# Low parts of the input weights made by an accumulating transfer in an encoder block on one core

## The chip, the core and the metric

The kernel runs on one core of one Trainium2 chip. A core has TensorE (PE in the profile, PEld for its weight loads), VectorE (DVE), ScalarE (ACT), GpSimd (POOL) and SyncE (SP), each with its own in-order instruction queue, and 16 transfer (DMA) engines that they share. The metric is the device time of one execution in microseconds; of several runs the median counts.

## The reference

One layer of a hybrid encoder block on 1,024 tokens of 1,024 channels, in float32:

```python
hn = rms_norm(h, ln_g[l])
proj = hn @ w_in[l] + b_in[l]            # 1024 -> 3584
glu_a, glu_b, z_conv, q, k, v, z_att = jnp.split(proj, cuts, axis=-1)
y_conv = conformer_conv(glu_a, glu_b, dw_w[l], ...)   # 31 taps, LayerNorm, swish, 512x512
y_att = neighbourhood_attention(q, k, v, rpb[l])      # 8 heads, window 8 x 16 on a 16 x 64 grid
y_conv = grouped_rms_norm(y_conv, ...) * silu(z_conv)
y_att = grouped_rms_norm(y_att, ...) * silu(z_att)
h = h + concatenate([y_conv, y_att]) @ w_out[l]
return rms_norm(h, final_g)
```

## The kernel before

Every large product is made in three matmuls of rounded operands (type fp32r): a float32 operand is split into a high part, its rounding, and a low part, the rest, and high x high + high x low + low x high are summed in PSUM (`proj`, L368). The split input `hi`, `lo` of the 1,024 tokens stays in SBUF.

The input projection is cut into 28 chunks of 128 output channels. A chunk's weights are 1,024 x 128 numbers, 512 KB. `prefetch` (L337) walks the chunks in the order `order` (L208): the first nine are the lead (three pairs for the gated linear unit of the convolution, then q, k and v of the first pair of heads), then come those that are worked in between attention blocks, and at the end two final gates (chunks 27 and 28 of the order). For each chunk it loads the raw weights from HBM on SP's queue (`wraw`, L210; eight pieces of 512 B for each partition), rounds them on ScalarE into the high part `wh` in two instructions of four 128-column blocks (KS = 4, L47), and subtracts on GpSimd, also in two instructions, to make the low part `wl` (`low_weight`, L355). There is one raw buffer (`r_raw`) and there are two buffers each for `wh` and `wl` (`r_w`), so a chunk's high part can be written when the last matmul of the chunk before the last one is done. The raw buffer is returned when the second subtraction is planned to end.

The program's order on every engine is written by a planner at build time (`Clock`, L95; `weave`, L110). It keeps a modelled time, adds a modelled cost for every instruction, and lets generators of higher priority go first whenever their modelled inputs are ready. The GpSimd subtractions wait in a list `jobs` and are issued when GpSimd's modelled queue is free. `ready[n]` holds a chunk's two tiles and the modelled time at which each of its eight blocks may be used; `weight` (L362) waits for it, and `proj` for each block's time. The taps of the depthwise convolution (`taps`, L470: one VectorE instruction a tap, with two operands in SBUF) fill VectorE wherever its modelled queue is empty. The real engines only keep the order, not the times.

`final_gates` (L1034) takes the last two chunks together: for each of the eight blocks the six matmuls of the one, then the six of the other. The output projection reads what the gates give, and its buffers are those that the gates release.

Of the kernel before, what the change touches and what calls it, by code (L numbers as in the profile page):

```python
# [9 lines left out]
F32 = mybir.dt.float32  # L10
F32R = mybir.dt.float32r
AF = mybir.ActivationFunctionType
ALU = mybir.AluOpType
# [4 lines left out]
P = 128  # L18
D = 1024
T = 1024  # L20
NK = D // P
# [25 lines left out]
KS = 4  # L47
# [7 lines left out]
QI = 0.1  # L55
LW = 10.9
SQ_DVE = (4,6)


def mk(t, offset, dims):  # L60
# [88 lines left out]
def block(ctx: ExitStack, tc: tile.TileContext, x, vecs, w_in, dw_w, pw_w, pw_b, rpb, w_out, final_g, out):  # L149
    nc = tc.nc  # L150
    pool = lambda name, bufs, **k: ctx.enter_context(tc.tile_pool(name=name, bufs=bufs, **k))
# [12 lines left out]
    ck = Clock(nc)  # L164
    ring = lambda n: Ring(ck, n)
    r_u, r_raw, r_w, r_x, r_uh, r_ul, r_gz, r_y = ring(16), ring(1), ring(2), ring(XB), ring(1), ring(0), ring(1), ring(1)
# [41 lines left out]
    order = [c + int(f[1:]) for f in LEAD + FILL for c in of[f[0]]] + [CH_ZC + 3, CH_ZA + 3]  # L208

    def wraw(n):  # L210
        c = order[n]
        raw = wrp.tile([P, NK, P], F32, tag="wr", name=f"wr{c}")
        nc.sync.dma_start(out=raw, in_=w_in[0][:, c * P:(c + 1) * P].rearrange("(k p) n -> p k n", p=P))
        return raw

    def wtiles(n):
        c = order[n]
        return (whp.tile([P, NK, P], F32R, tag="wh", name=f"wh{c}"),
                wlp.tile([P, NK, P], F32R, tag="wl", name=f"wl{c}"))

    for t in range(4):
        xload(t)
    raw0 = wraw(0)
    for t in range(4, NT):
        xload(t)
# [37 lines left out]
    def x_tile(t):  # L263
        yield land[t]
        ss = sm.tile([P, 1], F32, tag="ss", name=f"ss{t}")
        rs = sm.tile([P, 1], F32, tag="rs", name=f"rs{t}")
        eng = "dve" if t in SQ_DVE else "act"
        while t >= 4 and ck.q[eng] > ck.now + QI:
            yield ck.now + 0.1
        if t in SQ_DVE:  # L270
            e = ck.dve("scalar_tensor_tensor", out=acc[:, t % 4, :], in0=xt[t], scalar=1.0 / 1024.0, in1=xt[t],
# [57 lines left out]
    ready = {}  # L329
# [7 lines left out]
    def prefetch():  # L337
        for n in range(len(order)):
            if n < W_AHEAD or "pw" in state:
                yield from r_raw.get()  # L340
                raw, end = (wraw(n), ck.now + 4.0) if n else (raw0, land_w)
                yield from r_w.get()
            else:
                yield from r_w.get()
                yield from r_raw.get()
                raw, end = wraw(n), ck.now + 4.0
            whi, wlo = wtiles(n)
            yield end
            for k0 in range(0, NK, KS):
                kk = slice(k0, k0 + KS)  # L350
                t = ck.act(out=whi[:, kk, :], in_=raw[:, kk, :], func=AF.Copy)
                ck.jobs.append((t, partial(low_weight, n, raw, whi, wlo, kk)))
                yield

    def low_weight(n, raw, whi, wlo, kk):  # L355
        k = dict(out=wlo[:, kk, :], in0=raw[:, kk, :], in1=whi[:, kk, :].bitcast(F32), op=ALU.subtract)
        t = ck.gps("tensor_tensor", 0.1 + 0.0022 * KS * P, **k)
        ready.setdefault(n, (whi, wlo, []))[2].extend([t] * KS)
        if kk.stop == NK:
            r_raw.put(t)  # L360
# [628 lines left out]
    ck.spawn(all_turned(), 0)  # L989
    ck.spawn(tap_cols(), -1)  # L990
    ck.spawn(prefetch(), -1)
    ck.spawn(bias_rows(), 2)
    ck.spawn(lead(), 5)
# [221 lines left out]
_VECS = ["ln_g", "b_in", "dw_b", "cln_g", "cln_b", "gn_conv_g", "gn_att_g"]  # L1215
# [20 lines left out]
```

## Time and profile before

| | us |
|---|---|
| median of 3 runs | 571.23 (568.81 to 573.75) |
| the profiled execution | 572.21 |
| its span, first to last instruction | 570.4 |
| TensorE busy | 539.3 |
| VectorE busy | 412.2 |
| ScalarE busy | 260.1 |
| GpSimd busy | 195.1 |

TensorE's mean granted clock is 0.992 of full speed. Busy time is counted by instruction records; matmuls overlap, so one record of 0.39 us stands for about 0.23 us of progress where they follow each other closely. In the rows below a line gives the start and the duration in us, the engine, the line of the kernel, the operation, output and inputs, and in brackets the idle time before it and what ended that. L127, L131, L136, L140 and L144 are the helpers that record every matmul, transpose, activation, VectorE and GpSimd instruction, so groups go by the names of the tiles.

### The profile page before, as it was taken

To read this page: it belongs to the slowest core of one execution; us is meant where nothing else is said; L and a number is where in the kernel's file an instruction comes from. 1 tells how busy PE (TensorE), PEld (TensorE's weight loads), DVE (VectorE), ACT (ScalarE), POOL (GpSimd) and SP (SyncE) were. 2 spreads that over 40 slices of the span, in tenths; PEclk is the share of its full clock that TensorE was granted. 3 is DMA by queue.
4 is the path that set the end of the run, shared out by engine and by line. 5 is a ranking of instruction groups with operands and counts; after the bars stand their busy time and mean duration, and the time that the engine had idled before them with its cause. 6 is when DMAs were issued, how large, how long until landed. Compare 5 with 4: busy or idle time off the path is not lost.

```text
span 570.4 us, 7827 instructions
## 1 busy us (share of the span) xinstructions
PE 539.3 (95%) x2717; PEld 447.2 (78%) x2717; DVE 412.2 (72%) x665; ACT 260.1 (46%) x634; POOL 195.1 (34%) x176
## 2 busy tenths in 40 slices
PE   4999999898999998999997999999999999999995
PEld 3688888676888886888786788788888888888885
DVE  4747999987999979988999884667564365464232
ACT  6552221124555153655465645875665555253121
POOL 7513543232222343232525152542515552031121
PEclk9999999998999999999998999999999999999999
DMA  9413546663123442263241241101101470044221
GB/s 330 145 14 84 168 128 223 172 192 111 40 57 103 125 105 66 74 149 103 65 142 54 77 120 46 38 26 52 39 0 38 158 284 0 2 148 145 78 75 74
DMA packets 62331, 57.74 MB, mean 101 GB/s; under 512 B 9981, under 2 KB 51765, under 8 KB 62292
## 3 DMA queue, kind: packets, MB, share of 16 engines
q1 hardware_dynamic: 62222, 57.22, 33.6%
q8 instruction: 21, 0.34, 0.3%
q14 instruction: 18, 0.15, 0.1%
q10 hardware_dynamic: 70, 0.03, 0.0%
HBM read 36.58 MB, written 11.58 MB: 84 GB/s over the span
## 4 chain that ended last, share of the span: by engine, by line
PE 71%; DVE 17%; DMA 4%; issue 3%; ACT 2%; SPq 2%; POOL 1%; POOLq 0%; ACTq 0%; DVEq 0%
PE out L127 15%; PE pz L127 13%; DVE acc L140 12%; PE pv L127 6%; PE pk L127 6%; PE pq L127 5%; PE po L127 4%; PE pw L127 4%; PE pb L127 4%; PE ptp L131 3%; PE pa L127 3%; PE s L127 3%; DMA kl<-kl 1%; PE po L131 1%; DMA x<-in_x 1%
## 5 line engine op out<-in xcount | busy, mean ns | idle before, releaser
L140 DVE SCALAR_TENSOR_TENSOR acc<-glu,dwc,acc 128x512 f32<-128x512 f32 (+25 forms) x150 | 186.7, 1270 | 1.2
L144 POOL TENSOR_TENSOR wl<-wr,wh 128x512 fp32r<-128x512 f32 x56 | 93.9, 1695 | 153.0 <-ACT wh L136 147.7
L127 PE MATMUL pz<-hi,wh 128*128 128x512 f32 x128 | 52.2, 408 | 0.0
L127 PE MATMUL out<-wol,yh 128*128 128x512 f32 (+1 forms) x136 | 51.2, 377 | 0.0
L127 PE MATMUL out<-woh,yl 128*128 128x512 f32 (+1 forms) x136 | 51.2, 377 | 0.0
L127 PE MATMUL out<-woh,yh 128*128 128x512 f32 (+1 forms) x136 | 51.2, 377 | 0.0
L127 PE MATMUL pz<-hi,wl 128*128 128x512 f32 x128 | 50.3, 393 | 0.1
L127 PE MATMUL pz<-lo,wh 128*128 128x512 f32 x128 | 50.1, 391 | 0.0
L136 ACT ACTIVATE wh<-wr 128x512 fp32r<-128x512 f32 x56 | 32.3, 628 | 30.5 <-DMA wr<-in_w_in 20.9
L140 DVE TENSOR_TENSOR ptl<-ptp,pth 128x512 fp32r<-128x512 f32 x64 | 37.0, 614 | 1.2 <-ACT pth L136 1.2
L136 ACT ACTIVATE pth<-ptp 128x512 fp32r<-128x512 f32 x64 | 31.8, 543 | 13.2 <-PE ptp L131 12.4
L140 DVE CUSTOM_DVE_ANT_0 s<-s,bias 128x264 f32<-128x264 f32 (+1 forms) x64 | 30.2, 512 | 7.3 <-PE s L127 4.2
L140 DVE TENSOR_TENSOR xr<-out,xr 128x512 f32<-128x512 f32 (+1 forms) x17 | 11.1, 660 | 33.6 <-PE out L127 29.1
L136 ACT ACTIVATE prob<-s,mx 128x264 f32<-128x264 f32 (+1 forms) x64 | 33.6, 536 | 0.6 <-DVE mx L140 0.4
L136 ACT ACTIVATE os<-po 128x256 f32<-128x256 f32 x32 | 12.4, 387 | 41.9 <-PE po L127 41.8
L131 PE MATMUL ptp<-ident,prob 128*128 128x128 f32 x224 | 30.0, 273 | 0.0
L127 PE MATMUL pq<-hi,wh 128*128 128x512 f32 x64 | 26.6, 416 | 3.2 <-DVE v L140 3.2
L127 PE MATMUL po<-pth,v 128*128 128x256 f32 x112 | 29.5, 291 | 0.0
L144 POOL TENSOR_TENSOR ams<-ams,mhalf 128x8 f32<-128x8 f32 x8 | 14.6, 1819 | 43.5 <-DVE ams L140 43.5
L127 PE MATMUL po<-ptl,v 128*128 128x256 f32 x112 | 29.3, 290 | 0.0
L127 PEld LDWEIGHTS out<-woh,yh 128*128 128x128 f32 x136 | 25.6, 188 | 4.7
L127 PEld LDWEIGHTS out<-woh,yl 128*128 128x128 f32 x136 | 25.6, 188 | 4.7
(153 smaller groups left out, 1371.0 us busy)
## 6 DMA issues: line engine op xcount, KB each, us to landing
wr<-in_w_in SPq DMA_DIRECT2D x28, 512.0 KB
x<-in_x SPq DMA_DIRECT2D x8, 512.0 KB
wor<-in_w_out SPq DMA_DIRECT2D x8, 512.0 KB
xr<-in_x SPq DMA_DIRECT2D x8, 512.0 KB
out<-xr SPq DMA_DIRECT2D x16, 256.0 KB
kh<-kh SPq DMA_DIRECT2D x24, 128.0 KB
kl<-kl SPq DMA_DIRECT2D x24, 128.0 KB
q<-ql SPq DMA_DIRECT2D x16, 128.0 KB
```

The costliest lines, as they stand in the source:

```text
L127: self.nc.tensor.matmul(out, lhsT=lhsT, rhs=rhs, start=start, stop=stop)
L131: self.nc.tensor.transpose(out=out, in_=in_, identity=identity)
L136: self.nc.scalar.activation(**k)
L140: getattr(self.nc.vector, fn)(**k)
L144: getattr(self.nc.gpsimd, fn)(**k)
```

## The change

For the first three chunks nothing changes but the layout. From the fourth chunk on the raw buffer is returned right after the high part; ScalarE writes the negated high part into the low part's buffer, in two more instructions; and a transfer issued by GpSimd reads the chunk's weights from HBM a second time and adds them to that buffer. The planner is told 0.95 us for the issue and 5.8 us more until all eight blocks can be used. The host lays the weights out so that each partition of a chunk is one piece of 4 KB. The issue of the transfer goes to the head of the list `jobs`.

```diff
+N_SUB = 3
@@ wraw
-        nc.sync.dma_start(out=raw, in_=w_in[0][:, c * P:(c + 1) * P].rearrange("(k p) n -> p k n", p=P))
+        nc.sync.dma_start(out=raw, in_=w_in[c])
@@ prefetch
                 t = ck.act(out=whi[:, kk, :], in_=raw[:, kk, :], func=AF.Copy)
-                ck.jobs.append((t, partial(low_weight, n, raw, whi, wlo, kk)))
+                if n < N_SUB:
+                    ck.jobs.append((t, partial(low_weight, n, raw, whi, wlo, kk)))
                 yield
+            if n < N_SUB:
+                continue
+            r_raw.put(t)
+            for k0 in range(0, NK, KS):
+                kk = slice(k0, k0 + KS)
+                t = ck.act(out=wlo[:, kk, :], in_=whi[:, kk, :].bitcast(F32), func=AF.Copy, scale=-1.0)
+                yield
+            ck.jobs.insert(0, (t, partial(low_added, n, whi, wlo)))
+
+    def low_added(n, whi, wlo):
+
+        nc.gpsimd.dma_start(out=wlo, in_=w_in[order[n]], accum_op=ALU.add)
+        t = max(ck.q["pool"], ck.now) + 0.95
+        ck.q["pool"] = t
+        ready[n] = (whi, wlo, [t + 5.8] * NK)
@@ kernel
+    w_in = np.asarray(inputs["w_in"])[0].reshape(NK, P, -1, P).transpose(2, 1, 0, 3)
```

## Rows read from the trace of the kernel before

**Rows 1.** The page's parts 1 and 4: busy time by engine; the chain's shares.

```profile
PE 539.3 (95%) x2717; PEld 447.2 (78%) x2717; DVE 412.2 (72%) x665; ACT 260.1 (46%) x634; POOL 195.1 (34%) x176
...
PE 71%; DVE 17%; DMA 4%; issue 3%; ACT 2%; SPq 2%; POOL 1%; POOLq 0%; ACTq 0%; DVEq 0%
```

**Rows 2.** Timeline of TensorE, the waits for VectorE's results between 100 and 310 us.

```profile
101.17 0.49 PE L127 MATMUL pk<-hi,wh 128*128 128x512 f32 x1 [0.85 <-DVE ql L140]
...
108.55 0.50 PE L127 MATMUL pk<-hi,wh 128*128 128x512 f32 x1 [1.63 <-DVE ql L140]
...
127.32 0.36 PE L127 MATMUL s<-kl,q 128*128 128x264 f32 x1 [1.42 <-DMA kl<-kl]
...
220.56 0.48 PE L127 MATMUL pq<-hi,wh 128*128 128x512 f32 x1 [2.12 <-DVE v L140]
...
278.61 0.47 PE L127 MATMUL pq<-hi,wh 128*128 128x512 f32 x1 [1.07 <-DVE v L140]
...
307.56 1.09 PE L131 MATMUL ln<-ident,acc 128*128 128x128 f32 x8 [2.27 <-DVE ptl L140]
```

**Rows 3.** Busy time by stretch: PE, PEld, DVE, ACT, POOL, PEclk, DMA share, GB/s.

```profile
136.00:138.00 2.00, 2.00 (x7) 1.56 (x6) 2.00 (x7) 1.54 (x6) 0.00 (x0) 0.53 0.96 263
...
310.00:312.00 2.00, 1.62 (x6) 1.62 (x7) 1.93 (x7) 1.22 (x4) 0.72 (x2) 0.51 0.00 0
```

**Rows 4.** Chain (taps); GpSimd's timeline; stretch 45 to 345, low parts alone.

```profile
47.66 1.28 DVE acc L140
...
48.96 2.19 DVE acc L140
...
48.21 4.09 POOL L144 TENSOR_TENSOR wl<-wr,wh 128x512 fp32r<-128x512 f32 x2 [4.47 <-ACT wh L136]
...
45.00:345.00 300.00, 68.23 (x38) 0.99 0.41 113
```

**Rows 5.** Groups by line: busy us, mean ns of one | idle before.

```profile
L144 POOL TENSOR_TENSOR wl<-wr,wh 128x512 fp32r<-128x512 f32 x56 | 93.9, 1695 | 153.0 <-ACT wh L136 147.7 <-DMA row<-abn 5.2
...
L136 ACT ACTIVATE wh<-wr 128x512 fp32r<-128x512 f32 x56 | 32.3, 628 | 30.5 <-DMA wr<-in_w_in 20.9 <-PE pq L127 4.9 <-PE pz L127 4.6
```

**Rows 6.** Timelines of SP and ScalarE, two weight loads; then stretches as in rows 3.

```profile
43.77 0.40 SPq L213 DMA_DIRECT2D wr<-in_w_in  x1
...
47.50 1.15 ACT L136 ACTIVATE wh<-wr 128x512 fp32r<-128x512 f32 x2 [1.45 <-DMA wr<-in_w_in]
...
124.41 0.53 SPq L213 DMA_DIRECT2D wr<-in_w_in  x1
...
130.69 1.15 ACT L136 ACTIVATE wh<-wr 128x512 fp32r<-128x512 f32 x2 [4.18 <-DMA wr<-in_w_in]
...
43.00:48.00 5.00, 5.00 (x24) 4.14 (x23) 1.84 (x3) 1.19 (x2) 0.74 (x1) 1.00 0.41 110
...
455.00:460.00 5.00, 4.90 (x22) 3.70 (x21) 2.48 (x3) 3.66 (x7) 3.62 (x3) 1.00 1.04 415
```

**Rows 7.** Timelines, two chunks: high part's start and first matmul with the low part.

```profile
57.42 1.15 ACT L136 ACTIVATE wh<-wr 128x512 fp32r<-128x512 f32 x2 [0.49 <-DMA wr<-in_w_in]
...
67.37 0.39 PE L127 MATMUL pb<-hi,wl 128*128 128x512 f32 x1
...
279.63 1.15 ACT L136 ACTIVATE wh<-wr 128x512 fp32r<-128x512 f32 x2 [1.26 <-DMA wr<-in_w_in]
...
287.37 0.39 PE L127 MATMUL pz<-hi,wl 128*128 128x512 f32 x1
```

**Rows 8.** Timelines, the last chunk: high part, low part, first matmul with it.

```profile
454.30 1.15 ACT L136 ACTIVATE wh<-wr 128x512 fp32r<-128x512 f32 x2 [2.61 <-PE pz L127]
...
455.01 2.54 POOL L144 TENSOR_TENSOR wl<-wr,wh 128x512 fp32r<-128x512 f32 x2 [6.34 <-ACT wh L136]
...
456.36 0.51 PE L127 MATMUL pz<-hi,wl 128*128 128x512 f32 x1
```

**Rows 9.** The accumulator's instructions: duration ns min/median/max, first and last start.

```profile
L140 DVE TENSOR_SCALAR acc<-glu,dwc,cols x5: 535/802/811, 46.8 to 278.4; 128x1024 f32<-128x1024 f32 x3, 128x512 f32<-128x512 f32 x2
```

More of the change, by code (lines that the diff above doesn't have):

```diff
@@ L1224 @@
     nc = bacc.Bacc("TRN2", target_bir_lowering=False, num_devices=1)
-    inputs = dict(inputs, vecs=np.concatenate([np.asarray(inputs[n])[0].reshape(-1, P) for n in _VECS]))
+    w_in = np.asarray(inputs["w_in"])[0].reshape(NK, P, -1, P).transpose(2, 1, 0, 3)
+    inputs = dict(inputs, w_in=w_in, vecs=np.concatenate([np.asarray(inputs[n])[0].reshape(-1, P) for n in _VECS]))
     arrays, args = {}, []
```

## The prediction

> **What bounds the kernel now.** I read the page's first part first: TensorE is busy for 539.3 of 570.4 us, VectorE for 72% and the other engines for less [rows 1]. The chain that ended last lies on TensorE for 71% and on VectorE for 17% [rows 1]. So an edit moves the end only where TensorE stands still or runs at its lower clock, and the next view is the list of TensorE's waits in order of time. In the middle of the run they are waits for VectorE: 0.85 and 1.63 us for the low half of q, 1.42 us for copies of the low half of k (which VectorE writes), then 2.12, 1.07 and 2.27 us for v and for a low half of the probabilities [rows 2]. After two groups of such waits the granted clock is 0.53 and 0.51 of full speed, that is the 1.2 GHz level [rows 3]. Nothing there waits for a weight.
>
> The third view is VectorE's part of the chain, read beside GpSimd's timeline. A full-length convolution tap takes 1.28 us by itself, and 2.19 us where it runs beside the weights' low-part subtraction on GpSimd [rows 4]. The subtraction reads two operands from SBUF, and so does a tap. One pair of subtractions (4.09 us) hits two taps, which is 2 x 0.91 = 1.8 us of VectorE. Between 45 and 345 us, while the taps run, there are 38 subtractions, 19 pairs [rows 4]: up to 19 x 1.8 = 34 us of VectorE time in which it falls behind the order that the planner wrote.
>
> **Removed: 50 subtractions on GpSimd.** They are 50 of the 56 at a mean of 1.70 us, 85 us of GpSimd [rows 5], off the path by themselves. What counts is what they do to the taps. Without them VectorE is less late when the next q, k, v or probability piece is due. I take the first three waits (0.85 + 1.63 + 1.42 = 3.9 us) as gone: five or six pairs, about 10 us of collisions, come before them, several times their sum. Of the later three (5.5 us) I take two thirds, 3.6 us: a tap alone still costs 1.28 us against 1.15 us in the planner's formula (0.065 + 0.00106 x 1024, L139 to L141), so VectorE stays somewhat late. Each slow-clock stretch covers some 3 us at half rate, so 1.6 us lost; one of the two follows waits that I keep in part, so I count half of one, 0.8 us. Gain: 3.9 + 3.6 + 0.8 = 8.3 us. Its bounds are 4 us (only the first three) and 13 us (all six waits, 9.4, and both slow stretches, 3.2).
>
> **Added on ScalarE: 50 negating copies.** They have the form of the existing high-part copy, 0.63 us each [rows 5], so 31 us. ScalarE is busy for 46% [rows 1], and the four copies of a chunk stand together, 2.3 us in place of 1.15, ahead of a PSUM eviction or a softmax exponential. I price the queueing at nothing, because the bank being computed covers it (a half chunk is 24 matmuls of 0.23 us, 5.4 us). If that cover is gone in one chunk in ten, 25 x 1.15 / 10 gives 3 us.
>
> **Added on GpSimd's queue: 25 accumulating transfers.** The trace of before has no accumulating transfer and none issued by GpSimd. The planner carries 0.95 us for the issue and 5.8 us to the landing. Bounds from rows: a plain load of the same 512 KB reached its reader 3.7 us after its issue with the transfer engines 0.41 busy (43.77 to 47.50), and 6.3 us after it in a crowded stretch (124.41 to 130.69) [rows 6]. The accumulate moves the same bytes in and also reads its destination. So below: 3.7 us from issue. Above: 5.8 us stretched by 6.3/3.7, 9.9 us and 0.95 more. I take 0.95 + 5.8, near the middle. Behind the waiting issue on GpSimd stand only the small operations of norms, which had 2 x 1.7 us ahead of them before.
>
> The Trainium skill (DMA: Bandwidth & Descriptors, Anatomy of one DMA) fits about 2.0 us plus bytes over 436 GB/s for a transfer issued by GpSimd, an estimate of 3.2 us here. No row shows such a transfer. By that figure the last chunk's term below would be 2.6 us and the gate's 1.4 us smaller, and the kernel would end at 570 us.
>
> **What the longer preparation costs.** From the start of the high part to the landing a chunk now needs 1.15 + 1.15 + 0.1 + 0.95 + 5.8 = 9.15 us, where the subtraction took some 4 us. I compare it with what the trace leaves between the start of the high part and the first matmul that reads the low part:
>
> - In the dense start a chunk is 10.9 us of matmuls. The tightest is 57.42 to 67.37, 9.95 us [rows 7]; the following ones start right behind the freeing of their buffer and have 10.5 us or more. No stall at 5.8 us. If every landing took 2 us longer, every second chunk would stall by about 1 us.
> - The first attention gate has 279.63 to 287.37, 7.7 us [rows 7]: a stall of 9.15 - 7.74 = 1.4 us. The other chunks of the middle have 9 us or more, as far as I followed them.
> - The last chunk has no cover at all. Its buffer comes free with the last matmul of the chunk before, its high part starts at 454.30, its low part at 455.01, and TensorE already waits for it at 456.36 [rows 8]. The final gates take the last two chunks alternately, and the output projection can't start before the gates. Now: 454.30 + 2.30 + 0.1 + 0.95 + 5.8 = 463.45, so 7.1 us more. In that stretch the transfer engines are already full (share 1.04 between 455 and 460 [rows 6]), with the output weights and the second read of x, so I add 1.3 us, half of the 2.6 us by which the crowded load was longer. A standstill that long is followed by a slow stretch like those of [rows 3], 1.6 us. Sum: 10.0 us. Bounds: 4 + 1.6 = 5.6 with a plain load's time, 11 + 1.6 = 12.6 with the upper landing time.
>
> **Moved and re-laid.** The raw buffer is returned after the high part instead of after the subtraction, so raw loads on SP go out 3 to 4 us earlier; in the dense start the buffers for the high part come free later than the loads land, or nearly so, and this shifts traffic and no end. The weights are laid out on the host so that each partition reads 4 KB in one piece instead of eight of 512 B: nothing or some tenths, as few chunks wait for a load. The planner's changed times reorder some attention pieces; I price that at nothing with 3 us either way.
>
> **Sum.** The profiled execution took 572.2 us, 1.0 above the median 571.2. 572.2 - 8.3 (VectorE and clock) + 10.0 (last chunk) + 1.4 (first attention gate) = 575.3, less 1.0 gives 574 us.
>
> **Rivals.**
>
> - *Every landing is late* (slower). Place: the four chunks of the dense start, the middle's short chunks and the last one. For it: the transfer engines are above half busy for much of the stretch to 131 us, and the loads there were 6.3 us long. Against it: on chunks with 15 us and more of room nothing happens. It decides when issue plus landing passes about 8 us, where the last chunk costs its 12.6 us, the starts add some 3, the gate 3.5, and the gain shrinks to 7: 572.2 + 12.1 - 1.0 = 583 us.
> - *VectorE's relief wins* (faster). For it: 34 us of collisions against 9.4 us of waits; all six waits and both slow stretches could go, 12.6 us. With a landing like a plain load the last chunk costs 5.6 us and the gate nothing: 572.2 - 12.6 + 5.6 - 1.0 = 564 us. It decides when the landing is under about 4 us. Against it: GpSimd's attention-norm products and VectorE's own slower taps remain.
> - *GpSimd can't write its transfer while VectorE runs its faster instructions.* The only such form during the taps is the first tap of a block, 5 instructions of 0.80 us [rows 9]: at most 4 us, 578 us, and none of it in the last chunk, where VectorE works on two-operand forms. The Trainium skill (SBUF — State Buffer, SBUF: two separate sides) says that VectorE's two-port modes lock GpSimd out of writing descriptors, with a VectorE copy as its example; no run here shows that yet.
>
> **How the numbers follow.** A measurement of this kernel can tell about 1% from no change, 565.5 to 577 us. Forecast, the two big terms nearly cancel, with the third rival's small share: 0.50. Late landings: 0.29. Relief wins: 0.21. So faster 0.21, same 0.50, slower 0.29. The range reaches to 564 below, the full relief with a short landing, and to 584 above, the late landings and 1 us of reordering; under 2 in 10 is left out. The likeliest case alone runs from 568 to 580.
>
> **What would show it.** Right: taps of 2.19 us vanish from VectorE's rows after 56 us, the waits for ql, kl and v shrink to a third or less, and one standstill of TensorE of 7 to 10 us stands between the first matmuls of the final gates, with the granted clock near 0.5 behind it. Wrong: no such standstill (another chunk's order, or a landing of 3 us), stalls of over 1 us in each chunk between 56 and 100 us, or taps that stay slow because the transfers' issue collides with them as the subtraction did. If TensorE's waits for ScalarE grow by more than 3 us, the negating copies were not hidden.

## The result and the profile after

The changed kernel takes 607.0 us (median of 4 runs, 602.8 to 609.4) beside 571.9 for the kernel before on the same chip: ratio 1.061, 95% interval 1.054 to 1.069. That is slower than forecast (574) and above the range (564 to 584). The profiled execution took 602.8 us with a span of 601.0, so 30.6 us of span have to be found; the medians are 35 us apart.

The page of the changed kernel: parts 1 and 4 (busy time by engine, shares of the chain), and part 3 (queue: packets, MB, share of 16 engines' time).

```profile
PE 548.5 (91%) x2717; PEld 453.0 (75%) x2717; DVE 383.2 (64%) x665; ACT 286.5 (48%) x684; POOL 134.7 (22%) x151
...
q1 hardware_dynamic: 37134, 57.22, 30.9%
q0 software_dynamic: 3600, 13.11, 13.2%
...
PE 66%; DMA 11%; DVE 6%; SPq 6%; issue 4%; ACT 3%; POOL 2%; POOLq 0%; ACTq 0%; DVEq 0%
```

Against [rows 1] VectorE and GpSimd are less busy, as intended, and VectorE's share of the chain fell from 17% to 6%. Yet TensorE is idle for 52.5 us instead of 31.1, and the DMA's share of the chain rose from 4% to 11%. Most of VectorE's part of the chain went; transfers took its place.

The taps as a group (before, then changed), the changed kernel's instructions on the low parts (duration in ns min/median/max, first and last start in us), and the landing times of its transfers:

```profile
L140 DVE SCALAR_TENSOR_TENSOR acc<-glu,dwc,acc 128x512 f32<-128x512 f32 (+25 forms) x150 | 186.7, 1270 | 1.2
...
L142 DVE SCALAR_TENSOR_TENSOR acc<-glu,dwc,acc 128x512 f32<-128x512 f32 (+24 forms) x150 | 160.3, 1094 | 1.3
...
L138 ACT ACTIVATE wl<-wh x50: 612/616/633, 48.8 to 477.3; 128x512 fp32r<-128x512 f32 x50
L368 POOL DMA_DIRECT2D wl<-in_w_in x25: 858/875/1083, 50.3 to 478.2; - x25
...
DMA to landing us min/median/max: 5.3/6.1/10.2
```

The taps take 160 us where they took 187. The issue costs GpSimd 0.87 us. The landing is counted from the start of the issue, so the median transfer lands 5.2 us after its issue has ended: the two terms that the prediction took from the planner (0.95 and 5.8, 6.75 in sum) are a little above the measured 6.1.

TensorE's waits of the changed kernel, in order of time (start, duration, instruction, idle time before it and what ended it):

```profile
90.22 0.51 PE L129 MATMUL pq<-hi,wl 128*128 128x512 f32 x1 [0.42 <-DMA wl<-in_w_in]
104.23 0.76 PE L129 MATMUL pk<-hi,wl 128*128 128x512 f32 x1 [2.27 <-DMA wl<-in_w_in]
133.44 0.56 PE L129 MATMUL s<-kh,q 128*128 128x264 f32 x1 [5.46 <-DMA kh<-kh]
135.20 0.56 PE L129 MATMUL s<-kl,q 128*128 128x264 f32 x1 [1.20 <-DMA kl<-kl]
...
202.26 0.48 PE L129 MATMUL pv<-hi,wl 128*128 128x512 f32 x1 [1.92 <-DMA wl<-in_w_in]
208.49 0.56 PE L129 MATMUL s<-kh,q 128*128 128x264 f32 x1 [3.56 <-DMA kl<-kl]
...
483.82 0.77 PE L129 MATMUL pz<-hi,wl 128*128 128x512 f32 x1 [6.06 <-DMA wl<-in_w_in]
```

The waits of [rows 2] for q's low half and for v are gone. In their place stand four waits for an accumulated weight, the longest of them the standstill of the last chunk, and two groups for key copies. Behind or within the longer ones the granted clock is at or near half, the 1.2 GHz level. Busy time by stretch of the changed kernel, columns as in [rows 3]:

```profile
104.00:108.00 4.00, 3.77 (x10) 3.03 (x11) 3.12 (x3) 0.05 (x1) 0.64 (x1) 0.57 1.07 241
132.00:136.00 4.00, 1.36 (x4) 1.12 (x5) 0.20 (x1) 2.04 (x4) 0.88 (x1) 0.50 0.43 119
204.00:208.00 4.00, 0.93 (x3) 0.21 (x1) 0.37 (x1) 0.94 (x2) 0.00 (x0) 0.50 1.00 250
208.00:212.00 4.00, 2.75 (x11) 2.49 (x12) 1.59 (x6) 1.50 (x4) 0.86 (x1) 0.50 0.52 96
484.00:488.00 4.00, 4.00 (x10) 3.13 (x11) 1.16 (x4) 1.12 (x4) 0.00 (x0) 0.50 0.65 230
488.00:490.00 2.00, 2.00 (x6) 1.53 (x6) 0.00 (x0) 0.00 (x0) 0.00 (x0) 0.53 0.00 0
```

The wait of 2.27 us, in the 8th chunk, begins on GpSimd. The negating copies of that chunk end at 94.6 us, but ahead of the transfer's issue in GpSimd's queue stands a memset of a buffer for the position bias (`abn`), and GpSimd is idle for 11 us until an earlier transfer from that buffer has landed:

```profile
96.30 0.42 POOL L146 MEMSET abn<- 128x384 f32 x1 [11.01 <-DMA row<-abn]
96.83 0.86 POOL L368 DMA_DIRECT2D wl<-in_w_in  x1
```

The best guide to where time goes is the end of each chunk: the end of the last matmul that reads the chunk's low part, read from TensorE's timeline, minus the same in the kernel before. The table has it for all profiled kernels that the argument needs (us; minus means ahead of the kernel before; about 1 us at the start varies from one execution to the next).

| chunk (of 28) | after | 2nd run: accumulating, old order | 6th: plain transfer, old order | 4th: zeros, old order | 12th: zeros, new order | 3rd: subtraction, new order |
|---|---|---|---|---|---|---|
| 7 | +1.2 | +1.2 | +1.5 | +1.5 | +1.0 | +1.2 |
| 8 | +2.2 | -1.8 | -1.6 | -1.6 | -2.1 | +5.7 |
| 10 | +4.9 | +2.0 | -1.9 | -6.1 | -6.8 | +1.1 |
| 13 | +4.9 | +2.3 | -1.6 | -6.1 | -6.8 | +1.1 |
| 14 | +14.1 | +1.9 | -2.1 | -6.7 | -1.4 | +8.3 |
| 19 | +6.9 | +0.2 | -4.0 | -8.4 | -8.8 | +1.3 |
| 20 | +18.1 | -0.1 | -4.3 | -8.3 | +1.3 | +14.4 |
| 21 | +17.6 | +4.7 | -0.5 | -8.2 | -1.0 | +13.1 |
| 23 | +21.7 | +6.4 | +1.2 | -8.1 | +2.6 | +16.7 |
| 26 | +21.5 | +6.7 | +1.5 | -8.1 | +2.0 | +16.1 |
| 28 | +30.3 | +15.7 | +8.0 | -8.5 | +1.6 | +16.1 |

The stretch behind the last chunk, the output projection, is as long as before (94 us).

### The profile page after: what moved, and what is told of

It reads as the page before. It is cut to its first block, busy times and chain, and to the rows that moved or that the text cites. A ratio compares the mean times of both kernels' runs of the same rounds, so it can differ in the third digit from the quotient of the medians.

```text
span 601.0 us, 7870 instructions
## 1 busy us (share of the span) xinstructions
PE 548.5 (91%) x2717; PEld 453.0 (75%) x2717; DVE 383.2 (64%) x665; ACT 286.5 (48%) x684; POOL 134.7 (22%) x151
## 3 DMA queue, kind: packets, MB, share of 16 engines
q1 hardware_dynamic: 37134, 57.22, 30.9%
q0 software_dynamic: 3600, 13.11, 13.2%
## 4 chain that ended last, share of the span: by engine, by line
PE 66%; DMA 11%; DVE 6%; SPq 6%; issue 4%; ACT 3%; POOL 2%; POOLq 0%; ACTq 0%; DVEq 0%
PE out L129 15%; PE pz L129 11%; PE pk L129 7%; PE pq L129 5%; PE pv L129 5%; PE po L129 4%; PE pb L129 4%; PE pw L129 4%; PE ptp L133 3%; PE s L129 3%; SPq L466 3%; DMA kl<-kl 3%; DMA wl<-in_w_in 2%; DVE acc L142 2%; PE pa L129 2%
## 5 line engine op out<-in xcount | busy, mean ns | idle before, releaser
L142 DVE SCALAR_TENSOR_TENSOR acc<-glu,dwc,acc 128x512 f32<-128x512 f32 (+24 forms) x150 | 160.3, 1094 | 1.3
L368 POOL DMA_DIRECT2D wl<-in_w_in x25 | 22.6, 904 | 177.5 <-ACT wl L138 170.5
L142 DVE CUSTOM_DVE_ANT_0 s<-s,bias 128x264 f32<-128x264 f32 (+1 forms) x64 | 30.3, 512 | 19.2 <-PE s L129 18.6
L138 ACT ACTIVATE pth<-ptp 128x512 fp32r<-128x512 f32 x64 | 31.9, 543 | 16.1 <-PE ptp L133 16.0
L129 PEld LDWEIGHTS pz<-hi,wl 128*128 128x128 f32 x128 | 24.7, 193 | 12.0 <-issue 6.5
L142 DVE TENSOR_TENSOR xr<-out,xr 128x512 f32<-128x512 f32 (+1 forms) x17 | 11.1, 659 | 33.8 <-PE out L129 29.4
L142 DVE TENSOR_TENSOR ytok<-po,ytok 128x128 f32<-128x128 f32 x32 | 9.3, 289 | 36.3 <-ACT ytok L138 36.3
L129 PE MATMUL s<-kh,q 128*128 128x264 f32 (+1 forms) x64 | 23.1, 369 | 10.0 <-DMA kh<-kh 5.5
L133 PE MATMUL ptp<-ident,prob 128*128 128x128 f32 x224 | 31.3, 279 | 0.0
```

The costliest lines, as they stand in the source:

```text
L129: self.nc.tensor.matmul(out, lhsT=lhsT, rhs=rhs, start=start, stop=stop)
L133: self.nc.tensor.transpose(out=out, in_=in_, identity=identity)
L138: self.nc.scalar.activation(**k)
L142: getattr(self.nc.vector, fn)(**k)
L368: nc.gpsimd.dma_start(out=wlo, in_=w_in[order[n]], accum_op=ALU.add)
```

## The experiments

**First theory.** The change has four parts: the layout, the relief of VectorE, the accumulating transfer, and a changed order of TensorE's, VectorE's and SyncE's work. Runs 1 to 4 take them apart.

**1. Layout alone.** `N_SUB = 28` and the order of before.

```diff
-        nc.sync.dma_start(out=raw, in_=w_in[0][:, c * P:(c + 1) * P].rearrange("(k p) n -> p k n", p=P))
+        nc.sync.dma_start(out=raw, in_=w_in[c])
```

> All 28 chunks keep the subtraction on GpSimd; only the weights' layout in HBM is the changed one (4 KB pieces). Order of every engine as in the kernel before. My prediction's step: nothing or some tenths, 570 to 572 us. Rival (the layout itself does harm or good through the transfer engines): more than 3 us to either side.

571.9 us, ratio 1.0015 (0.9994 to 1.0037). The layout costs and gives nothing that these runs can tell; 25,000 fewer packets change no end here.

**2. Accumulating transfers in the order of before.** The planner is told the subtraction's times, so that TensorE's, VectorE's and SyncE's orders are those of before to the line.

```diff
+            if n >= N_SUB:
+                for k0 in range(0, NK, KS):
+                    kk = slice(k0, k0 + KS)
+                    nc.scalar.activation(out=wlo[:, kk, :], in_=whi[:, kk, :].bitcast(F32), func=AF.Copy, scale=-1.0)
+    def low_added(n, raw, whi, wlo, kk):
+        if kk.stop == NK:
+            nc.gpsimd.dma_start(out=wlo, in_=w_in[order[n]], accum_op=ALU.add)
+        t = ck.queue("pool", 0.1 + 0.0022 * KS * P, None)
```

> The accumulating transfers and the negating copies of the changed kernel, but TensorE, VectorE and SP keep exactly the instruction order of the kernel before (the planner is told the subtraction's times). Theory A, the loss of 35 us is mostly the planner's new order: this kernel lands near my sum, 572 to 578 us, with one standstill of 7 to 10 us at the final gates. Theory B, the loss is real waiting, landings of up to 10 us and k copies behind the transfers: 595 us or more here too.

588.9 us, ratio 1.033 (1.030 to 1.036): between the two theories, so neither holds alone. The loss stands in three places. TensorE's waits of this run:

```profile
129.08 0.36 PE L129 MATMUL s<-kh,q 128*128 128x264 f32 x1 [3.30 <-DMA bias<-row]
131.49 0.56 PE L129 MATMUL s<-kl,q 128*128 128x264 f32 x1 [2.04 <-DMA kl<-kl]
...
347.73 0.38 PE L129 MATMUL s<-kl,q 128*128 128x264 f32 x1 [2.67 <-DMA kh<-kh]
...
470.20 0.76 PE L129 MATMUL pz<-hi,wl 128*128 128x512 f32 x1 [6.07 <-DMA wl<-in_w_in]
```

At attention's start, at the gather of the last key chunk, and in the last chunk. Only the last one waits for the accumulated weight itself. At attention's start TensorE waits for the small transfers of the position bias and the keys. The chain of waits of this run there (start, length, what), and below it two stretches of this run, attention's start and the gather of the last key chunk:

```profile
112.25 6.40 DMA row<-abn
...
119.20 6.86 DMA bias<-row
...
126.07 5.28 DMA kl<-kl
```

```profile
88.00:136.00 48.00, 41.19 (x169) 32.65 (x168) 32.47 (x35) 14.56 (x28) 4.22 (x6) 0.93 0.81 221
338.00:346.00 8.00, 6.99 (x31) 5.20 (x29) 3.95 (x7) 2.65 (x6) 3.72 (x4) 1.00 0.96 196
```

Three transfers of 48 to 128 KB, one after the other, take 5.3 to 6.9 us each. The transfer engines are 0.81 busy at attention's start and 0.96 at the gather. The kernel before, the chain there and the same two stretches:

```profile
110.90 4.94 DMA row<-abn
...
116.44 3.70 DMA kl<-kl
```

```profile
88.00:136.00 48.00, 41.84 (x178) 32.84 (x177) 43.31 (x40) 10.90 (x23) 17.09 (x10) 0.98 0.59 176
338.00:346.00 8.00, 8.00 (x41) 6.57 (x40) 4.87 (x11) 2.52 (x6) 4.00 (x5) 1.00 0.62 154
```

**3. The new order with the subtraction.** TensorE, VectorE and SyncE issue exactly what they issue in the changed kernel, in its order; the low part is made by GpSimd as before.

```diff
-        nc.gpsimd.dma_start(out=wlo, in_=w_in[order[n]], accum_op=ALU.add)
+        for k0 in range(0, NK, KS):
+            kk = slice(k0, k0 + KS)
+            nc.gpsimd.tensor_tensor(out=wlo[:, kk, :], in0=raw[:, kk, :], in1=whi[:, kk, :].bitcast(F32), op=ALU.subtract)
```

> The instruction order of the changed kernel on TensorE, VectorE and SP, but the low parts are made by GpSimd's subtraction as before: no accumulating transfer, no negating copy. Theory A (order): 590 us or more, with attention as late as in the changed kernel. Theory B (transfers): 575 us or less. Both in part: 580 to 588 us.

590.1 us, ratio 1.035 (1.031 to 1.038): the order, which the prediction priced at nothing with 3 us either way, loses 19 us without a single accumulating transfer. TensorE's waits of this run:

```profile
106.17 0.79 PE L129 MATMUL pk<-hi,wh 128*128 128x512 f32 x1 [4.62 <-DVE ql L142]
...
202.29 0.56 PE L129 MATMUL s<-kh,q 128*128 128x264 f32 x1 [3.96 <-DMA kh<-kh]
204.28 0.56 PE L129 MATMUL s<-kl,q 128*128 128x264 f32 x1 [1.43 <-DMA kh<-kh]
```

The first of them is VectorE's lateness, 4.62 us where it was 0.85 and 1.63 [rows 2]. The others are the first scores of the next pair of heads, which this order puts ahead of the 14th chunk: their key copies aren't there yet.

**4. GpSimd reads nothing.** The order of before, zeros written in place of the low parts.

```diff
+        if n < 3:
+            t = ck.gps("tensor_tensor", 0.1 + 0.0022 * KS * P, **k)
+        else:
+            t = ck.gps("memset", 0.1 + 0.0022 * KS * P, ap=wlo[:, kk, :].bitcast(F32), constant=0.0)
```

> Order and work of the kernel before, but from the fourth chunk on GpSimd fills the low part with zeros instead of subtracting, so it reads nothing from SBUF (the low parts of the weights are left out of the result; TensorE does the same matmuls). Measures the term VectorE's relief by itself: the prediction took 8.3 us, bounds 4 and 13, so 563 us (559 to 568). Rival: the waits for VectorE have other causes, 570 us or more. Taps of 2.19 us should be gone in either case.

562.4 us, ratio 0.986 (0.984 to 0.989): 8.35 us under the 570.7 of the kernel before on the same chip, against 8.3 in the prediction. This run's groups by line:

```profile
L142 DVE SCALAR_TENSOR_TENSOR acc<-glu,dwc,acc 128x512 f32<-128x512 f32 (+25 forms) x150 | 160.7, 1097 | 1.2
L146 POOL MEMSET wl<- 128x512 f32 x50 | 25.3, 531 | 130.1 <-PE pq L129 40.7 <-PE pb L129 30.0 <-PE pk L129 25.1
```

GpSimd still writes 50 tiles, at the same steps, and the taps are as fast as in the changed kernel. Of the full-length taps that overlap such a write, twelve take 1.26 to 1.28 us, as a tap does alone; one takes 1.90, and it also overlaps a product of GpSimd with two inputs. So it is GpSimd's reading beside a two-operand tap that costs, and not its writing. The Trainium skill (SBUF — State Buffer, SBUF: two separate sides) says the same: an instruction of VectorE with two SBUF inputs contends only with a GpSimd operation that reads SBUF.

**What these leave open.** Whether the loss of run 2 comes from the bytes or from the accumulation; what the last chunk is worth in the changed kernel; which number of the planner turns the order.

**5. The last two chunks subtract.** Changed kernel with `if n < N_SUB or n >= 26:` at both places.

> The changed kernel with the subtraction back in the last two of the 28 chunks only; all other chunks keep the accumulating transfer. In the changed kernel's trace the lag behind the kernel before grows from +21.5 us at the end of the 26th chunk to +30.3 at the end of the 28th. Theory (the last low part is a serial step of load, two sets of copies, issue and 6 us of landing with nothing after it to cover it): these 8.7 us go, 607.0 - 8.7 = 598 us, and the wait of 6.06 us on the weight's transfer in the last chunk is gone. Rival (the last chunk's late end is inherited from the order and from full transfer engines ahead of it): under 3 us, 604 or more.

595.3 us, ratio 1.040 (1.037 to 1.044), 11.8 under the changed kernel's median (on another chip; the ratios are 2.1% apart, some 12 us); in the profiled executions the lag at the last chunk is 20.9 instead of 30.3, so 9.4 us. The wait of 6.06 us is gone. The last chunk is a serial step, as forecast.

**6. The same bytes without the addition.** Run 2 with a plain transfer.

```diff
-            nc.gpsimd.dma_start(out=wlo, in_=w_in[order[n]], accum_op=ALU.add)
+            nc.gpsimd.dma_start(out=wlo, in_=w_in[order[n]])
```

> The order of before with the negating copies and one transfer of the weight from GpSimd's queue per chunk, as in the second experiment (588.9 us), but the transfer writes the weight instead of adding it: the subtraction itself is left out, and the low part holds the weight. Same bytes read from memory, no read of the tile and no addition. Theory (it is the accumulation that takes the transfer engines, about 1.9 times the engine time per MB of the plain transfers: 3.2 us of all 16 for one chunk): landing falls from 6.1 to about 4 us or less, the waits of attention's start and of the last chunk shrink, 575 to 581 us. Rival (it is the 13 MB that are read a second time, or the issue and the copies in front): landing stays above 5 us and the time within 586 to 590.

580.0 us, ratio 1.013 (1.010 to 1.016), inside the theory's 575 to 581. Queue and landing of this run:

```profile
q0 software_dynamic: 3600, 13.11, 7.6%
...
DMA to landing us min/median/max: 3.5/4.7/7.8
```

7.6% of 578.8 us over 25 transfers is 1.76 us of all 16 engines for 512 KB. In the changed kernel it is 13.2% of 601.0 over 25, 3.17 us, and in run 2 12.9% of 586.4, 3.03. The accumulation nearly doubles the transfer's load on the engines. At the 10th chunk, just behind attention's start, the lag goes with that load: -6.1 us with no second transfer, -1.9 with 1.76 us a chunk, +2.0 with 3.03. The landing's median was expected at 4 us or less and is 4.7, so that part of the theory missed, and the last chunk still costs 6.5 us. At the end run 2 is 24.2 us behind run 4, which has neither transfers nor copies; run 6 is 16.5 behind it. So about two thirds of what the mechanism costs in the old order are the second transfer as such, with the negating copies in front of it, and one third is the addition; by the ratios it is 2.7% and 2.0%.

**7. Four accumulating transfers.** Run 2 for the 4th to 7th chunk only, subtraction elsewhere: `partial(low_added if 3 <= n < 7 else low_weight, ...)`.

> The order of before, the accumulating transfer only for the fourth to the seventh chunk, the subtraction for all others. The three largest waits of the kernel before on these chunks' low parts and queries (0.85 + 1.63 + 1.42 us) and some of the small ones should go, and the attention's start is left as it was: theory 566 to 568 us, faster than before (570.7). Rival (the accumulating transfers of the dense start crowd out loads that are due there, or the relief of VectorE is worth little in these four chunks): 570 to 573.

568.3 us, ratio 0.993 (0.991 to 0.995): 0.7% less than before, clear of the interval; just above the expected 566 to 568 in time, inside it by the ratio (this chip's kernel before takes 571.75). The two waits for q's low half are gone; one of 1.67 us for an accumulated weight came (landing in this crowded start: 7.1 us median).

**8 and 10. Two numbers of the planner.** Run 8 loads the raw weight ahead for 14 chunks instead of 12; run 10 tells the planner a landing of 2.0 us, while the transfer stays what it is.

```diff
-W_AHEAD = 12
+W_AHEAD = 14
```

```diff
-        ready[n] = (whi, wlo, [t + 5.8] * NK)
+        ready[n] = (whi, wlo, [t + 2.0] * NK)
```

> The changed kernel with one number of the planner changed: the raw weight is loaded ahead of a free weight slot for the first 14 chunks instead of the first 12. In the changed kernel the planner takes the weight of the 14th chunk for late, puts the scores of the next pair of heads ahead of it, and TensorE then stands 5.5 and 3.6 us on key copies; the 20th chunk starts 18 us late behind it. Theory (this one late weight starts the cascade): the order around the 14th chunk goes back to that of before, the lag at the 20th chunk falls from +18 to under +8, and the time to 590 to 597 us. Rival (later chunks, whose raw weight still isn't loaded ahead, each bring such a turn of the order): 602 to 607.

> The changed kernel with one number of the planner changed: it is told that the transfer lands 2.0 us after its issue and not 5.8; the transfers themselves are the same. TensorE's order then differs from that of before in 1208 lines of an ordered comparison instead of 2466. Theory (the planner's measured landing alone turned the order, and the order costs 16 to 18 us): 590 to 597 us. Rival (the order was turned mostly by what precedes the landing: the two sets of copies, the slot handed back earlier and the job put ahead of the others): 602 to 608.

Run 8: 600.6 us, ratio 1.051 (1.046 to 1.056). The lag at the 14th chunk falls from 14.1 to 9.4 us, but at the 20th it is still +15.0 where the theory wanted under 8. That one late weight starts the whole cascade is refuted. Run 10: 595.2 us, ratio 1.043 (1.038 to 1.049), inside the theory's 590 to 597. The landing that the planner was told, though about right, makes the kernel 10 to 12 us slower (by the ratios and by the medians) than a wrong, shorter one. It isn't all: 588.9 would be the order of before, and the lag at the 20th chunk still jumps from +1.9 to +10.5. Nor is the order half way back, as the count of lines in the expectation suggests: compared by the tiles' names in the traces, TensorE's 2,717 matmuls differ from those of before in 655 lines (both sides counted) for the changed kernel, 625 for run 8 and 637 for run 10. Which of the other edits turns the rest (the raw buffer returned earlier, the job put first in the list, the times of the copies) wasn't tried.

**9 and 11. Accumulating where the table shows no loss.** Old order; run 9: 4th to 7th and 12th to 19th chunk; run 11: all of run 2's but the 8th to 11th, the 22nd (its transfer is the one issued at 337 us) and the last two.

```diff
+            if 3 <= n < 7 or 11 <= n < 26 and n != 21:
```

> The order of before; the accumulating transfer for the 4th to 7th and the 12th to 19th chunk (twelve of them), the subtraction for the chunks whose transfers would fall on attention's start, on the gather of the last key chunk, and for the rest. Theory: the gain of the run with four (568.3 us, 0.993 of before) stays and the middle adds the wait of 2.1 us of the 15th chunk that went in the run with all 25: 565 to 567 us. Rival (transfers crowd each other in the middle too): 569 to 573.

> The order of before; accumulating transfers in eighteen chunks: all of the second experiment's 25 (588.9 us) but the 8th to 11th, the 22nd and the last two. Theory (the loss of that experiment lies in three places: about 8 us where four transfers fall on the loads of attention's start, 5 where the one issued at 337 us falls on the gather of the last key chunk, 9 in the last two chunks): all three go, and with them some relief of VectorE in these chunks: 565 to 569 us. Rival (each accumulating transfer costs a little everywhere): 575 or more.

Run 9: 567.9 us, ratio 0.995 (0.992 to 0.997), just above the theory's 565 to 567 and no better than run 7. Run 11: 569.7 us, ratio 0.999 (0.996 to 1.002), just above the theory's 565 to 569, and far from the rival's 575. Its profiled execution, 567.3 us, is the fastest of its twelve; in it the lag at the 10th chunk is -5.9 us (run 2: +2.0), at the 21st -7.3 (+4.7) and at the last -5.4 (+15.7). The two stretches in run 11, the second shifted by 8.4 us, by which its gather of the last key chunk comes earlier than in run 2:

```profile
88.00:136.00 48.00, 47.01 (x211) 38.08 (x210) 43.81 (x46) 13.92 (x30) 16.06 (x10) 1.00 0.68 207
329.60:337.60 8.00, 8.00 (x38) 6.41 (x38) 4.05 (x9) 1.58 (x3) 4.24 (x5) 1.00 0.62 163
```

At the gather the transfer engines are back at 0.62, the share of before, and TensorE doesn't stop.

So seven of 25 transfers carry the whole loss of run 2. The other eighteen come out even (0.999), which is less than the four of run 7 (0.993).

**12. The new order by itself.** Run 3 with zeros in place of the subtraction.

```diff
-            nc.gpsimd.tensor_tensor(out=wlo[:, kk, :], in0=raw[:, kk, :], in1=whi[:, kk, :].bitcast(F32), op=ALU.subtract)
+            nc.gpsimd.memset(wlo[:, kk, :].bitcast(F32), 0.0)
```

> The changed kernel's order on TensorE, VectorE and SyncE, and GpSimd writes zeros in place of the low parts from the fourth chunk on (they are left out of the result): no subtraction beside VectorE's taps, no accumulating transfer, no late landing. Compared with the fourth experiment (the same zeros in the order of before, 562.4 us) it gives the price of the order by itself. Theory (the order costs its price whatever the low parts are made by, 16 to 19 us): 578 to 582 us. Rival (the order is only bad with late inputs, the standstill of 4.6 us on a low half of q in the third experiment being VectorE slowed by the subtraction): 563 to 570 us.

572.9 us, ratio 1.003 (1.001 to 1.006): between both expectations, so neither held. Against run 4 the order alone costs 1.003 - 0.986 = 1.7%, some 10 us; against run 3, the subtraction in this order costs 17 us where it costs 8 in the old. Part of the 19 us of run 3 was VectorE's lateness, which the new order bears less well: TensorE waits for VectorE for 19.6 us in run 3 and 11.1 in run 12, for 14.4 before and 9.8 in run 4. In run 3 SyncE's loads into the raw buffer also wait for the subtraction (99.6 us in 13 waits), with whatever stands behind them in its queue; in run 12 mostly for ScalarE, and what that difference adds wasn't taken apart. The 10 us stand at the 14th chunk (lag -6.8 to -1.4) and at the 20th (-8.8 to +1.3). The 20th chunk starts right behind the same pair's scores in this run and in the changed kernel:

```profile
318.73 0.37 PE L129 MATMUL s<-kh,q 128*128 128x264 f32 x1
...
320.11 0.48 PE L129 MATMUL pk<-hi,wh 128*128 128x512 f32 x1
```

```profile
335.50 0.37 PE L129 MATMUL s<-kh,q 128*128 128x264 f32 x1
...
336.88 0.48 PE L129 MATMUL pk<-hi,wh 128*128 128x512 f32 x1
```

Before, they are at 317.44 and 318.81, 13.5 us after the end of the 19th chunk (305.29). In run 12 the 19th chunk ends 8.8 us earlier, at 296.46, and the 20th starts 1.3 us later: 23.7 us with nothing for TensorE but attention and its waits. By the traces 58 matmuls of attention stand between the two chunks in the order of before and 104 in the new one: it did the projections' chunks earlier and attention's pieces later, and here the one has to wait for the other. Run 12, between the two chunks:

```profile
296.00:320.00 24.00, 18.32 (x105) 15.55 (x105) 20.77 (x46) 17.01 (x44) 8.20 (x9) 0.86 0.21 73
```

TensorE is busy for 18.3 of 24 us at 0.86 of its clock.

## Why the prediction was wrong

The account of the profiled executions, from the table: relief of VectorE -8.5 us (run 4); the order by itself +10.1 (run 12 minus run 4, 1.6 + 8.5); then what the transfers add in this order, with their negating copies (changed kernel minus run 12): +4 up to the 8th chunk, +7.5 at attention's start to the 10th, +4 at the 14th, +4 in the middle, +9 in the last two chunks. That is some 30 us, the lag that the table ends with. The medians are some 4.5 us further apart, which it doesn't cover; the profiled execution of the changed kernel is the fastest of its four.

- **VectorE's relief, 8.3 us: right.** Run 4 measured 8.35. Its parts differ a little: TensorE's waits for q, k, v and the probabilities' low halves [rows 2] and one of 0.6 beside them fell from 10.0 to 3.7 us in sum in run 4, of which 2.6 are the waits for the probabilities that were to shrink to a third and didn't. The collisions behind them were 26 us of taps (186.7 less 160.3) where the prediction had up to 34. The first slow stretch is gone (clock 1.00 from 100 to 140 us, where it was 0.96), the second is milder (0.92 from 300 to 314 us, where it was 0.88).
- **The transfer's own time, 0.95 + 5.8 us: right, a little long** (0.87 and a median of 5.2, 6.1 together). From the start of the high part to the landing the median is 8.9 us where the prediction had 9.15. So the rival in which every landing is late isn't what happened: some are (the maximum is 10.2 us), most aren't. The Trainium skill's fit for a transfer issued by GpSimd (DMA: Bandwidth & Descriptors, Anatomy of one DMA) gave an estimate of 3.2 us. The fastest plain one of run 6 took 3.5 us, so the trace comes near it for a plain transfer at its best; the median plain one took 4.7, and the fastest accumulating one of the changed kernel 5.3.
- **The last chunk, 10.0 us: right in the sum.** 9.4 us by run 5's profile, 11.8 by its median. As forecast, TensorE stands still and then runs at a clock of 0.50. The parts are off in opposite directions: the standstill is 6.06 us, where the sum had 8.4 and the sign 7 to 10, and the slow stretch is about 6 us long (0.50 to 0.53), some 3 us lost where the sum had 1.6.
- **The first attention gate, 1.4 us: wrong**, and small. No wait for a low part stands between 210 and 460 us, in the changed kernel or in run 2. In run 2, with the order of before, the chunk at that gate had 8.6 us from its high part to the first matmul that reads the low part, and the transfer landed after 7.7.
- **The dense start, no stall: right** to the 6th chunk, and nearly for the 7th, which waits 0.42 us. The 8th waits 2.27 us, and the clock behind it is 0.57. The prediction looked at what stands behind the issue on GpSimd, and not at what stands ahead of it: the memset that waits for a transfer.
- **Negating copies at nothing: not contradicted.** TensorE's waits for ScalarE are 4.2 us in sum (2.1 for outputs, 1.7 for norms, 0.4 other), as before. No run had the copies alone, so what they cost by way of other engines stays in the transfers' share.
- **The first step that failed: the transfer was priced by when it lands, and not by what it takes from others.** The prediction had the row: the stretch to 131 us is crowded [rows 6]. It used it to lengthen the weight's own landing and for the last chunk. It never asked which transfers the new ones delay. 25 transfers at 3.2 us of all engines, nearly twice the engine time per byte of the plain ones, are added, and four of them fall on a chain of small dependent transfers at attention's start. That costs 8 us (run 2 minus run 4 at the 10th chunk, the negating copies included), and 5 more at the last key chunk (12.9 minus 8.2 at the 21st). By run 11, both go when seven transfers go, together with the last chunk's loss.
- **The second step that failed: "The planner's changed times reorder some attention pieces; I price that at nothing with 3 us either way."** It measured +10 us alone, and with late inputs more. No row of the kernel before could give it. But the diff showed that three times in the planner change (a longer way to the low part, the raw buffer returned sooner, the job put first), and that this decides the order of everything behind. An order not seen needs a bound in proportion to what it rules, not 3 us.
- **The rival of GpSimd locked out: not met.** The issue took 0.86 to 1.08 us, 25 times, most of them beside taps and other two-operand forms; none of them ran beside the first tap of a block, so the changed kernel doesn't test it.

What stays open: the +4 us in the middle between the 14th and the 26th chunk, which are spread over small waits, the 4.5 us by which the medians are further apart than the profiled executions, the share of the negating copies, and which of the planner's other edits turns the order at the 20th chunk.

## What to carry to other kernels

Price an added transfer three times: its own landing, the time that it takes from the engines that all transfers share, and the chain of small dependent transfers that runs beside it; the last is where it cost most here (8 and 5 us in the old order). When a change alters the times that a static planner works with, run the old order with the new mechanism and the new order with the old mechanism before judging either: here the mechanism that frees VectorE is worth 8 us, in four chunks 0.7% net, and the order and the shared engines ate the rest several times over. A time that is about right, told to a greedy planner, need not give a better order.

## What the runs showed of the hardware that was not expected

An accumulating transfer of 512 KB took 3.17 us of all 16 transfer engines, a plain one from the same queue 1.76 us (run 6), and the plain loads of SyncE's queue about 1.7 us (30.9% of 601.0 us for 57.22 MB, scaled to 512 KB). Its fastest landing, from the start of the issue, was 5.3 us, that of the plain one 3.5. GpSimd writing beside VectorE's two-operand taps slowed them by nothing (mean 1097 ns with 50 tiles of zeros, 1094 with none), while GpSimd reading two operands took the mean to 1270.
